# v from scaled raw x, the inverse rms behind its products, the shift's share behind attention, and h made later

## The chip, the cores and the metric

The kernel runs on one core of a Trainium2 chip. A core has TensorE (PE in the profile, its weight loads PEld), VectorE (DVE), ScalarE (ACT), GpSimd (POOL) and SyncE (SP, which issues most DMAs); each runs its own instructions in order, and semaphores tie them together. The metric is the time of one execution on the device in microseconds, the median of several.

## The reference

One layer of an encoder over 512 positions of width 1024 (DEPTH and BATCH are 1). What bears on the change is the head of it and one branch:

```python
mod = silu(c) @ w_c + b_c                      # 3 x 1024
shift, scl, gate = split(mod, 3)
h = rms_norm(x, g_pre) * (1.0 + scl) + shift   # 512 x 1024
proj = h @ w_in                                # 512 x 8192
xa, za, q, k, v, zb, ga, gb = split(proj)      # 1024 columns each
y_b = neighbourhood_attention(q, k, v, rpb) * silu(zb)
```

rms_norm multiplies each row of x by one number, the inverse of its root mean square. The other branch (a convolution, two recurrences over the positions), the two sigmoid gates, the three output products w_pa, w_pb, w_o and a last rms_norm follow. All is float32; the kernel makes a float32 product from three products of numbers split in a high and a low part (high x high, high x low, low x high), each rounded to the form that TensorE takes at full speed.

## The kernel before

`Plan` holds a list of operations, each with its engine, an estimated cost, the tiles it reads and writes and a rank. `Plan.run` emits them engine by engine: the lowest rank among those that can begin about now by its estimates. What it emits is the order of each engine's instructions; on the chip they run in that order and wait for their data. `HEAD` (line 44) gives ranks by name to the operations of the beginning. Tiles come from fixed sets of slots (36 of 128x512, 32 of 128x1024, eight PSUM banks).

The beginning, in the order of the data:

- `par_sb` (line 405) holds c and the small parameters; its DMA is issued by ScalarE. Line 409 to 417 make silu(c) in it and transpose it; line 437 writes silu(c), broadcast to 128 rows, into two PSUM banks `cbs` by 16 products; `silr` is its copy in SBUF (line 380, a helper for all copies and casts).
- `xT` (line 470) is x turned, features on partitions, four tiles of two feature slices each, loaded in two halves of 256 positions. Squares (line 483), their sums over slices (486, 490), the sums over partitions by products with ones (496) and `rstd_ops` (464 to 462) give the inverse rms of each position; line 513 broadcasts it to all partitions (`rb`, `rbs`).
- `modulate(k)` loads for each of eight feature slices k two tiles of w_c (`wc`) and reduces them against silu(c): scale `scs[k]`, with g_pre in it, and shift `shs[k]`. Slice 0 has forms of its own (551, 555), slice 1 reads PSUM in halves (566), the others read `silr` (571).
- `make_h(k)`: ht = xT x scale x inverse rms (584, 595), hh = ht + shift rounded (587, 598), hl the rest of it (589, 600).
- `split_v(k)`: `wv`, the rows of w_in that make v, as `vh` and `vl` (380, 620, 383).
- `vmm`: v in eight units, two halves of 512 columns times four blocks of 128 positions (`VU`), each in a PSUM bank `vps`; 8 units x 8 slices x 3 products = 192 products (line 386, a helper for all such products), slice by slice. `fill` (504) puts short products in TensorE's way before them, so that it isn't idle.
- `vout` (676, 677, 680): v is split in high and low and written to DRAM (`vscr`), from where attention loads it in another order (`load_v`).

Then `proj` makes one tile of 128 columns x 512 positions of any of the other projections: a load of 0.5 MB (`wraw`), a cast (`whi`, line 380), a subtraction (`wlo`, 383) and 24 products with hh and hl. For the first head pairs the order is q, k and the gate z; each further one follows in the same way. `bias` (738) makes the bias tables on POOL. `scores` and `attend` run for two head pairs at a time between the products of later projections. At its end `attend` writes the inverse sums of the softmax to DRAM and reads them back broadcast (905, 908, `rcx`), multiplies them into the gate sz (909), multiplies that by the attention output yt (911), and splits the result in `ybh` and `ybl` for the products with w_pb, which come after all attention. `gate_of` and `main` tie loads to the progress of TensorE.

## Time and profile before

| what | us |
|---|---|
| three timed runs | 558.68, 558.93, 559.44 |
| median | 558.93 |
| span of the profiled execution, from its first to its last instruction | 556.93 |
| TensorE busy in the span | 548.6 |
| VectorE, ScalarE, POOL busy | 388.4, 320.1, 102.1 |
| moved by DMA | 82.54 MB |

The profiled execution has no time of its own beside its span; the difference to the timed runs, about 2 us, is what lies before the first and behind the last instruction. A row of the timeline gives the start in us from the span's beginning, the duration in us (of several like instructions together, "x16"), the engine, the line, the operation, what it writes <- what it reads, the shapes, and in brackets the idle time ahead of it and who ended it. A row by groups gives the count, the total in us, the mean in ns and the idle time. SPq and ACTq are the instructions with which SP and ScalarE issue DMAs.

### The profile page before, as it was taken

The numbers are of one execution on the slowest core, as the hardware profiler recorded it, in microseconds if no ns is written. First come the engines' busy times: TensorE is split into PE (matmuls) and PEld (weight loads), VectorE is DVE, ScalarE is ACT, GpSimd is POOL, SyncE is SP. The second block draws the span as 40 slices with busy tenths as digits, with TensorE's granted clock in tenths as the row PEclk, the third lists the DMA queues.
The fourth block names the chain that finished last, engine by engine and source line by source line (L and its number), as shares of the span: only waits on it lengthen the run. The fifth ranks groups of instructions, "written<-read, shape, count | busy, mean of one in ns | idle before, by whom it ended". The sixth has DMA issues, their size and how long they took to land.

```text
span 556.9 us, 7643 instructions
## 1 busy us (share of the span) xinstructions
PE 548.6 (99%) x2769; PEld 458.8 (82%) x2769; DVE 388.4 (70%) x707; ACT 320.1 (57%) x557; POOL 102.1 (18%) x98
## 2 busy tenths in 40 slices
...
GB/s 294 408 408 124 299 302 198 155 191 54 148 202 67 123 200 114 4 95 190 78 123 159 31 122 167 41 114 62 89 100 376 130 76 75 152 301 1 0 38 115
DMA packets 30825, 82.54 MB, mean 148 GB/s; under 512 B 4548, under 2 KB 5700, under 8 KB 30788
## 3 DMA queue, kind: packets, MB, share of 16 engines
...
q14 instruction: 15, 0.12, 0.1%
HBM read 75.60 MB, written 6.44 MB: 147 GB/s over the span
## 4 chain that ended last, share of the span: by engine, by line
PE 99%; DVE 0%; POOL 0%; issue 0%; ACT 0%; POOLq 0%
PE acc L386 79%; PE hx L386 8%; PE pv L386 3%; PE pt L848 2%; PE sp L386 2%; PE gt L386 2%; PE hx L504 1%; PE hx L437 1%; PE hd L551 0%; PE hd L496 0%; PE hd L513 0%; DVE yo L1215 0%; DVE yo L1183 0%; DVE xr L1187 0%; ACT sd L1205 0%
## 5 line engine op out<-in xcount | busy, mean ns | idle before, releaser
L386 PE MATMUL acc<-hhl,whi 128*128 128x512 f32 x784 | 243.1, 391 | 0.0
L386 PEld LDWEIGHTS acc<-hhl,whi 128*128 128x128 f32 x784 | 145.7, 188 | 29.2
L386 PE MATMUL acc<-hhl,wlo 128*128 128x512 f32 x392 | 152.9, 390 | 0.0
L386 PEld LDWEIGHTS acc<-hhl,wlo 128*128 128x128 f32 x392 | 73.6, 188 | 15.5
L380 ACT CAST whi<-wraw 128x1024 fp32r<-128x1024 f32 x72 | 74.4, 1045 | 1.8 <-DMA wraw<-in_w_in_dram 0.9
L1194 POOL TENSOR_TENSOR yo<-yo,gfin 128x512 f32<-128x512 f32 x6 | 8.1, 1350 | 337.8 <-ACT xr L1191 337.7
L383 POOL TENSOR_TENSOR wlo<-wraw,whi 128x1024 fp32r<-128x1024 f32 x23 | 56.0, 2438 | 64.0 <-ACT whi L380 32.1
L383 DVE TENSOR_TENSOR wlo<-wraw,whi 128x1024 fp32r<-128x1024 f32 x49 | 59.2, 1220 | 2.3 <-ACT whi L380 2.1
L386 PE MATMUL acc<-woh,mhl 128*128 128x512 f32 (+1 forms) x144 | 40.4, 366 | 0.0
L386 PE MATMUL acc<-ybhl,whi 128*128 128x512 f32 x128 | 39.4, 390 | 0.0
L386 PE MATMUL acc<-yahl,whi 128*128 128x512 f32 x128 | 39.4, 390 | 0.0
L738 POOL TENSOR_TENSOR nb<-msk,braw 128x192 f32<-128x192 f32 (+1 forms) x48 | 30.7, 670 | 27.8 <-DMA braw<-in_rpb_dram 26.7
L837 ACT ACTIVATE p<-p,mn 128x192 f32<-128x192 f32 (+1 forms) x64 | 30.4, 478 | 6.7 <-DVE mn L830 6.6
L1079 DVE SCALAR_TENSOR_TENSOR gm<-gm,acc 128x512 f32<-128x512 f32 x16 | 11.0, 688 | 33.0 <-PE acc L386 33.0
L386 PE MATMUL hx<-vh,hhl 128*128 128x512 f32 x112 | 33.5, 389 | 0.0
L830 DVE CUSTOM_DVE_ANT_0 p<-sp,nb 128x192 f32<-128x192 f32 (+1 forms) x64 | 31.4, 602 | 0.6 <-PE sp L386 0.2
L386 PEld LDWEIGHTS acc<-woh,mhl 128*128 128x128 f32 x144 | 26.1, 189 | 4.4
L985 DVE SCALAR_TENSOR_TENSOR xc<-acc,prm,xc 128x511 f32<-128x511 f32 (+1 forms) x24 | 18.0, 750 | 14.9 <-ACT xc L978 14.3
L386 PEld LDWEIGHTS acc<-ybhl,whi 128*128 128x128 f32 x128 | 24.0, 188 | 5.0
L386 PEld LDWEIGHTS acc<-yahl,whi 128*128 128x128 f32 x128 | 24.0, 188 | 5.0
L386 PE MATMUL acc<-wol,mhl 128*128 128x512 f32 (+1 forms) x72 | 26.4, 366 | 0.0
L386 PE MATMUL acc<-yahl,wlo 128*128 128x512 f32 x64 | 24.9, 390 | 0.0
...
## 6 DMA issues: line engine op xcount, KB each, us to landing
wraw<-in_w_in_dram SPq DMA_DIRECT2D x56, 512.0 KB, 5.0
wc<-in_w_m_dram SPq DMA_DIRECT2D x22, 512.0 KB, 10.1
...
vscr<-va SPq DMA_DIRECT2D x8, 512.0 KB, 4.3
wraw<-in_w_pb_dram SPq DMA_DIRECT2D x8, 512.0 KB, 3.5
wraw<-in_w_pa_dram SPq DMA_DIRECT2D x8, 512.0 KB
wo<-in_w_o_dram SPq DMA_DIRECT2D x8, 512.0 KB, 5.2
wv<-in_w_v_dram SPq DMA_DIRECT2D x7, 512.0 KB
```

The lines of the kernel that those rows point to most:

```text
L380: return lambda e: nc.scalar.copy(o(), i()) if e == "ACT" else nc.vector.tensor_copy(o(), i())
L383: return lambda e: ENGINE[e].tensor_tensor(o(), a(), b().bitcast(F32), op=ALU.subtract)
L386: nc.tensor.matmul(o, a, b, start=first, stop=last)
L437: nc.tensor.matmul(cb.ap[:, k * P:(k + 1) * P], ident.ap[:, 4 * n + k:4 * n + k + 1].to_broadcast([P, P]), par_sb.ap, start=True, stop=True)
L504: op("PE", 0.3, lambda e: nc.tensor.matmul(wb.ap[:, :P], onesc.ap, onesc.ap, start=True, stop=True), 5000 + j, r=[onesc], hold=[wb], until ...
L738: nc.gpsimd.tensor_tensor(o, mv, view, op=ALU.subtract)
L830: nc.vector.tensor_tensor_reduce(out=o, in0=v(spv(h, e)[:, :nk]), in1=v(nb[:, h, :nk]), scale=1.0, scalar=3e38, op0=ALU.add, op1=ALU.min, ...
L837: nc.scalar.activation(pv2(i), pv2(i), AF.Exp, bias=mn.ap[:, c:c + 1], scale=-1.0, accum_out=sm.ap[:, 4 * h + b:4 * h + b + 1])
L848: nc.tensor.transpose(ptp.ap[:, j * P:(j + 1) * P], pt_.ap[:, j * P:(j + 1) * P], ident.ap)
L985: nc.vector.scalar_tensor_tensor(a, b, wcol, a, op0=ALU.mult, op1=ALU.add)
L1079: op("DVE", dve(512), lambda e: nc.vector.scalar_tensor_tensor(t.ap, t.ap, 1.0, o.ap, op0=ALU.add, op1=ALU.mult), n - 1.9, r=[o], rw=[t], ...
L1194: op(("DVE", "POOL"), (dve(w), pool_(w)), lambda e: ENGINE[e].tensor_tensor(y(), y(), gfin[n].ap[:, gs], op=ALU.mult), rank + 0.1, r=[gfin ...
```

## The change

v is no longer made from h. With r the inverse rms of a position, scale' = g_pre x (1 + scl) and s the shift, h = r x (x scale') + s, so v = r x (x scale') @ w_v + s @ w_v. The first part needs no r until after its products; the second is one number per column of v and, since the weights of the softmax sum to one, the same number per column of the attention output.

- `split_x(k)`: hx = xT x scale' rounded, lx the rest; the products of v take these. `modulate` is split in scale (m = 1) for all slices, then shift (m = 0); both are one reduction 1024 wide that reads silu(c) from two PSUM banks side by side (`pair`). The special forms of slices 0 and 1 go.
- The squares are now taken of x itself, positions on partitions: four tiles `xn` of 0.5 MB are loaded for it, ScalarE squares and sums each; root, reciprocal and one Newton step give r in `rxc`, one column per block of 128 positions. It is turned, written to DRAM and read back broadcast as `rbs` by two DMAs that ScalarE issues. The products of line 496, 513 and 551 go.
- `make_h` comes behind all that: POOL multiplies xT by `rbs` (ht), ScalarE applies scale and shift (hs) and rounds (hh), VectorE subtracts (hl).
- `split_v`: 512-wide casts; the subtractions of the second half (k > 0) go to POOL.
- Six of the eight units of v run slice by slice; the last two run all eight slices after them.
- `vout`: r is multiplied in while v is split, on ScalarE by its scale operand, on VectorE in two passes 256 wide.
- The shift's share: shift is turned, written to DRAM and read back broadcast (`shr`); for each head pair a turned tile `wvt` of w_v (0.5 MB, a new input) is loaded and reduced against it (`v_bias`). In `attend` szr and yb become ytr = yt x rcx and yb = (ytr + share) x sz.
- x_t is stored so that each load of `xT` is one of 0.5 MB. `HEAD` is new; `AFTER` is empty; `Plan` counts DMA at slightly other rates.

```diff
+    "mod11": -17.3886, "lx1": -17.2743, "vh31": -17.0702, "wv0": -16.5875, "wc01": -16.1285, "x0": -16.0517,
+    "hx0": -15.3174, "wv1": -15.269, "vl21": -15.2314, "rn": -15.1384, "lx2": -15.1381, "lx6": -15.0948,
+    "sq0": -15.0022, "vl30": -14.9726, "mod21": -14.9726, "rv": -14.958, "vh20": -14.9549, "vh01": -14.8259,
+    "rd": -14.8255, "hx1": -14.8111, "vl00": -14.7926, "rxs": -14.7914, "hx2": -14.7913, "sq2": -14.7906,
+    "vh10": -14.7903, "sq1": -14.7846, "vh11": -14.7845, "vl01": -14.7726, "wc11": -14.1485, "wv2": -14.1485,
+    "xn0": -14.1484, "hx7": -13.8386, "vl20": -13.755, "xn1": -13.425, "wc21": -13.4246, "x1": -11.5502,
+    "wv3": -10.6407, "wc31": -10.6405, "wv4": -10.6403, "x2": -10.6403, "wc41": -10.0318, "wc51": -9.4608,
+    "mod51": -9.2919, "xn3": -9.2864, "vl41": -8.7911, "vl60": -8.7248, "mod01": -8.5793, "rr": -8.5792,
+    "mod41": -8.579, "mod71": -8.5634, "vl31": -8.5632, "wlo11": -8.4861, "lx4": -8.3642, "mod61": -8.3639,
+    "lx0": -8.3637, "vl61": -8.3098, "wlo10": -8.3032, "lx3": -8.1603, "hx4": -8.1298, "mod31": -8.1233,
+    "vh70": -7.9037, "wv5": -7.7231, "hx6": -7.7091, "vl10": -7.6401, "silr1": -7.4727, "vh71": -7.4726,
+    "xn2": -7.4663, "wc61": -7.4659, "vh21": -7.3661, "whi11": -7.366, "wv6": -7.347, "hx5": -7.1954, "x3": -7.1314,
+    "vh60": -7.1263, "hx3": -7.1056, "vh50": -7.0646, "vh61": -7.0642, "silr0": -6.7343, "sq3": -6.7223,
+    "voh": -6.5563, "rxl": -6.4074, "vh41": -6.4073, "vh00": -6.4, "vh30": -6.0598, "vh40": -5.3971,
+    "wc71": -4.8311, "w10": -4.7451, "wv7": -4.6289, "wc10": -4.6288, "wc60": -4.6039, "vh51": -4.1781,
+    "wc00": -3.7535, "w9": -3.6762, "wc30": -3.6235, "wc20": -3.548, "w11": -3.1239, "wc70": -3.1235,
+    "wc50": -2.8074, "wc40": -2.807, "vl71": -2.4421, "vl11": -2.1401, "ht0": -2.1401, "ht3": -2.0073,
...
+    pair = ps.tile([P, 1024], F32, name="pair")
+
     def B(cls):
-        return pl.tile(cls, lambda i: ps.tile([P, 512], F32, tag=f"b{i}", name=nm(cls)))
+        return pl.tile(cls, lambda i: pair[:, 512 * i - 1024:512 * i - 512] if i in (2, 3) else ps.tile([P, 512], F32, tag=f"b{i}", name=nm(cls)))
...
-    xTp = {(j, i): xT[j].part(i * 512, i * 512 + 512) for i in range(2) for j in range(4)}
-    for i in range(2):
-        for j in range(4):
-            load(xTp[j, i], whole(xTp[j, i]), x_t[i, j], -19.9 + 0.4 * i + 0.1 * j, 262144, name=f"x{i}{j}")
+    for j in range(4):
+        load(xT[j], whole(xT[j]), x_t[j], -19.9 + 0.1 * j, 524288, spare=2, name=f"x{j}")
+
+    ssx, rxc, rxt = const("ssx", [P, NT]), const("rxc", [P, 32]), T("rxt")
+    op("POOL", 0.1, lambda e: nc.gpsimd.memset(rxc.ap, 1.0), 0, w=[rxc])
+    for t in range(NT):
+        xn = W("xn")
+        load(xn, whole(xn), x[t * P:(t + 1) * P, :], 0, 524288, spare=2, name=f"xn{t}")
+        op("ACT", act(1024, 0, True), lambda e, xn=xn, t=t: nc.scalar.activation(xn.ap, xn.ap, AF.Square, accum_out=ssx.ap[:, t:t + 1]), 0,
+           rw=[xn], w=[ssx], name=f"sq{t}")
+    rv, rsd, rrc, rq = (C(f"{g}2", NT, 1) for g in ("v", "sd", "r", "q"))
+
+    def newton(e):
+        nc.vector.tensor_tensor(rq.ap, rrc.ap, rrc.ap, op=ALU.mult)
+        nc.vector.tensor_tensor(rq.ap, rq.ap, rv.ap, op=ALU.mult)
+        nc.vector.scalar_tensor_tensor(rxc.ap[:, :NT], rq.ap, -3.0, rrc.ap, op0=ALU.add, op1=ALU.mult)
+        nc.vector.transpose(rxt.ap[:, :32], rxc.ap)
+
+    op("ACT", 0.29, lambda e: nc.scalar.activation(rsd.ap, ssx.ap, AF.Sqrt, bias=epsc.ap), 0, r=[ssx, epsc], w=[rsd], name="rd")
+    op("DVE", 0.17, lambda e: nc.vector.tensor_scalar(rv.ap, ssx.ap, D * EPS, None, op0=ALU.add), 0, r=[ssx], w=[rv], name="rv")
+    op("DVE", 0.17, lambda e: nc.vector.reciprocal(rrc.ap, rsd.ap), 0, r=[rsd], w=[rrc], name="rr")
+    op("DVE", 0.8, newton, 0, r=[rrc, rv], rw=[rxc], w=[rq, rxt], lock=True, name="rn")
+
+    def turned(scr):
+
+        return bass.AP(scr.tensor, scr.offset, [[32, 4], [P, 32], [1, 32]])
+
+    xscr = pl.fixed(dp.tile([32, P], F32, name="xscr"))
+    op("ACT", 0.5, lambda e: nc.scalar.dma_start(turned(xscr.ap), rxt.ap[:, :32]), 0, r=[rxt], w=[xscr], late=3.0, name="rxs")
+    rbs = T("rbs")
+    op("ACT", 0.5, lambda e: nc.scalar.dma_start(rbs.ap, bass.AP(xscr.ap.tensor, xscr.ap.offset, [[0, P], [1, 512]])), 0, r=[xscr], w=[rbs],
+       late=4.0, name="rxl")
...
+    hx, lx, hh, hl = {}, {}, {}, {}
+    vh, vl = {}, {}
+    shc, sht = const("shc", [P, 32]), T("sht")
+
+    def sil():
+        assert [cb.slot for cb in cbs] == [2, 3]
+        return pair
+
+    zero = op("POOL", 0.1, lambda e: nc.gpsimd.memset(shc.ap, 0.0), -18.5, w=[shc])
+
+    def modulate(k, m):
+
+        t, r = W("wc"), C("sc", 1, 10) if m else shc.part(k, k + 1)
+        (scs if m else shs)[k] = r
+        b = mods.ap[:, 8 + k:9 + k] if m else pc(16 + k, 17 + k)
+        g = mods.ap[:, k:k + 1] if m else 0.5
+        load(t, whole(t), w_m[3 * k + m], k - 5, 524288, spare=2, name=f"wc{k}{m}")
+        op("DVE", dve(1024) + 0.08, lambda e: nc.vector.tensor_tensor_reduce(
+            out=t.ap, in0=t.ap, in1=sil(), scale=g, scalar=b, op0=ALU.mult, op1=ALU.add, accum_out=r.ap),
+           k - 1.5, r=cbs + [mods, prm], rw=[t], w=[r], after=[zero], name=f"mod{k}{m}")
+
+    def split_x(k):
+
+        hx[k], lx[k] = two("xhl")
+        xk = lambda: xT[k // 2].ap[:, k % 2 * 512:k % 2 * 512 + 512]
+        op("ACT", act(512, 1), lambda e: nc.scalar.activation(hx[k].ap, xk(), AF.Copy, scale=scs[k].ap), k - 1.19,
+           r=[xT[k // 2], scs[k]], w=[hx[k]], name=f"hx{k}")
+        op("DVE", dve(512), lambda e: nc.vector.scalar_tensor_tensor(
+            lx[k].ap, xk(), scs[k].ap, hx[k].ap.bitcast(F32), op0=ALU.mult, op1=ALU.subtract), k - 1.18,
+           r=[xT[k // 2], hx[k], scs[k]], w=[lx[k]], lock=True, name=f"lx{k}")
...
+        xk = lambda: xT[k // 2].ap[:, k % 2 * 512:k % 2 * 512 + 512]
+        op("POOL", pool_(512), lambda e: nc.gpsimd.tensor_tensor(t.ap, xk(), rbs.ap, op=ALU.mult), k - 1.2, r=[xT[k // 2], rbs], w=[t], name=f"ht{k}")
+        op("ACT", act(512, 2), lambda e: nc.scalar.activation(t.ap, t.ap, AF.Identity, scale=scs[k].ap, bias=shs[k].ap), k - 1.195,
+           r=[scs[k], shs[k]], rw=[t], name=f"hs{k}")
+        op("ACT", act(512), cast(whole(hh[k]), whole(t)), k - 1.19, r=[t], w=[hh[k]], name=f"hh{k}")
+        op("DVE", dve(512), sub(whole(hl[k]), whole(t), whole(hh[k])), k - 1.18, r=[t, hh[k]], w=[hl[k]], lock=True, name=f"hl{k}")
...
+        t, z = W("wv"), (slice(0, S), slice(S, D))
+        load(t, whole(t), w_v[k], k - 4.5, 524288, spare=2, name=f"wv{k}")
+        (h0, l0), h1, l1 = two("vhl"), T("vh", F32R), T("vl", F32R)
+        for n, hi, lo in ((0, h0, l0), (1, h1, l1)):
+            vh[k, n], vl[k, n] = (hi, whole(hi)), (lo, whole(lo))
+            op("ACT", act(512), lambda e, hi=hi, n=n: nc.scalar.copy(hi.ap, t.ap[:, z[n]]), k - 1.1, r=[t], w=[hi], name=f"vh{k}{n}")
+            op(*(("POOL", pool_(512)) if k and n else (("DVE", "POOL"), (dve(512), pool_(512)))), sub(whole(lo), lambda n=n: t.ap[:, z[n]], whole(hi)), k - 1.09, r=[t, hi],
+               w=[lo], lock=True, name=f"vl{k}{n}")
 
     for k in range(KD):
-        modulate(k)
-        wv_load(k)
+        modulate(k, 1)
+        split_x(k)
+        split_v(k)
+    for k in range(KD):
+        modulate(k, 0)
         make_h(k)
...
-                mm(vps[u].ap, (hl if p == 2 else hh)[k].ap[:, ts], (vl if p == 1 else vh)[k, n][1](),
+                mm(vps[u].ap, (lx if p == 2 else hx)[k].ap[:, ts], (vl if p == 1 else vh)[k, n][1](),
                    k == 0 and p == 0, k == KD - 1 and p == 2)
-        th, tl = (hhp[t // 2], hlp[t // 2]) if k == 0 else (hh[k], hl[k])
+        th, tl = hx[k], lx[k]
...
+        for j, parts in enumerate(([0], [1], [2]) if k < 2 else ([0, 1], [2]) if k < KD - 1 else ([0, 1, 2],)):
+            for m, u in enumerate(VU[:6]):
+                ops.append(vmm(u, k, parts, k + 0.1 * j + 0.01 * m))
         main.append(ops[0])
         if k == 0:
-            fill(ops[12], vps[VU[2]])
+            fill(ops[5], vps[VU[5]])
+    for m, u in enumerate(VU[6:]):
+        ops = [vmm(u, k, [0, 1, 2], 8 + 0.2 * m + 0.01 * k) for k in range(KD)]
...
-        op("ACT", act(512), lambda e: nc.scalar.copy(view(0, 192), src()), rank, r=[vps[u]], w=[a], name="voh")
-        op("DVE", dve(512), lambda e: nc.vector.tensor_tensor(view(64, 64), src(), view(0, 192).bitcast(F32), op=ALU.subtract),
-           rank, r=[vps[u]], rw=[a], name="vol")
+        rs = rxc.ap[:, t:t + 1]
+        op("ACT", act(512, 1), lambda e: nc.scalar.activation(view(0, 192), src(), AF.Copy, scale=rs), rank, r=[vps[u], rxc], w=[a], name="voh")
+        def low(e):
+            for b in range(2):
+                o, i1 = (a.ap.rearrange("p (g c) -> p g c", g=4)[:, :, c:c + 64] for c in (64 + 64 * b, 192 * b))
+                nc.vector.scalar_tensor_tensor(o, src()[:, :, b, :], rs, i1.bitcast(F32), op0=ALU.mult, op1=ALU.subtract)
+        op("DVE", 2 * dve(256), low, rank, r=[vps[u], rxc], rw=[a], name="vol")
...
+    sscr = pl.fixed(dp.tile([32, P], F32, name="sscr"))
+    op("DVE", 0.2, lambda e: nc.vector.transpose(sht.ap[:, :32], shc.ap), 7, r=[shc], w=[sht], name="sht")
+    op("SP", 0.5, lambda e: nc.sync.dma_start(turned(sscr.ap), sht.ap[:, :32]), 8, r=[sht], w=[sscr], size=16384, late=SLACK, name="shs")
+    shr = W("shr")
+    load(shr, whole(shr), bass.AP(sscr.ap.tensor, sscr.ap.offset, [[0, P], [1, D]]), 8, 524288, r=[sscr], spare=3, name="shr")
+    cv = const("cv", [P, KD])
+    cvs = [cv.part(i, i + 1) for i in range(KD)]
+
+    def v_bias(pr, rank, after):
+
+        t = W("wvt")
+        load(t, whole(t), w_vt[pr], rank - 2, 524288, after=after, spare=5, name="wvt")
+        op("DVE", dve(1024) + 0.08, lambda e: nc.vector.tensor_tensor_reduce(
+            out=t.ap, in0=t.ap, in1=shr.ap, scale=0.5, scalar=0.0, op0=ALU.mult, op1=ALU.add, accum_out=cvs[pr].ap), rank,
+           r=[shr], rw=[t], w=[cvs[pr]], lock=True, name="cv")
...
-        op("DVE", dve(512), lambda e: nc.vector.tensor_tensor(rbc(sz.ap), rbc(sz.ap), nat(rcx.ap), op=ALU.mult),
-           pos - 0.3, r=[rcx], rw=[sz], lock=True, name="szr")
-        op("DVE", dve(512), lambda e: nc.vector.tensor_tensor(rbc(sz.ap), nat(yt.ap), rbc(sz.ap), op=ALU.mult), pos + 0.5, r=[yt],
-           rw=[sz], lock=True, name="yb")
+        v_bias(pr, pos + 0.2, gate_of(len(main), 2))
+        op("DVE", dve(512), lambda e: nc.vector.tensor_tensor(rbc(rct.ap), nat(yt.ap), nat(rcx.ap), op=ALU.mult),
+           pos + 0.4, r=[yt, rcx], rw=[rct], lock=True, name="ytr")
+        op("DVE", dve(512), lambda e: nc.vector.scalar_tensor_tensor(sz.ap, rct.ap, cvs[pr].ap, sz.ap, op0=ALU.add, op1=ALU.mult),
+           pos + 0.5, r=[rct, cvs[pr]], rw=[sz], lock=True, name="yb")
```

More of the change, by code (lines that the diff above doesn't have):

```diff
@@ L44 @@
 HEAD = {
[22 rows of a table removed]
-AFTER = [('wc71', 'wc41')]
[25 rows of a table added]
+}
+AFTER = []
 class Tile_:
@@ L334, in layer @@
 @with_exitstack
-def layer(ctx, tc, x, x_t, par, w_m, w_v, w_in, w_blk, rpb, amask, w_pa, w_pb, w_o, g_final, out):
+def layer(ctx, tc, x, x_t, par, w_m, w_v, w_vt, w_in, w_blk, rpb, amask, w_pa, w_pb, w_o, g_final, out):
     nc = tc.nc
```

156 lines of the change are left out of this document (4 added, 152 removed), and 30 rows, old and new, of the table HEAD.

## The prediction, made before the changed kernel was run

> **What bounds the kernel now.** First the page: its share of busy time and the chain that ended last.
>
> ```profile
> span 556.9 us, 7643 instructions
> PE 548.6 (99%) x2769; PEld 458.8 (82%) x2769; DVE 388.4 (70%) x707; ACT 320.1 (57%) x557; POOL 102.1 (18%) x98
> PE 99%; DVE 0%; POOL 0%; issue 0%; ACT 0%; POOLq 0%
> ```
>
> TensorE carries 99% of the chain, so the same chain in order of time is read next (start, us, what), to see which of its pieces are work and which only fill time.
>
> ```profile
> 5.09 2.99 PE hx L437 x16
> 8.08 2.46 PE hx L504 x22
> ...
> 16.34 44.23 PE hx L386 x192
> 60.57 19.49 PE acc L386 x86
> ...
> 397.22 152.89 PE acc L386 x696
> 550.11 0.02 issue
> ```
>
> Three stretches. Up to 16 us TensorE is busy, but with warm-up products (L504) and small products that prepare the inputs. Then come the 192 products of v until 60.57 us, then everything else until 550.1 us, back to back. One product of the projections costs 19.49/86 = 0.2266 us; 192 at that rate are 43.5 us. So the v stage, which takes 44.47 us from its first product at 16.10 (below) to 60.57, loses only 1.0 us. The kernel gains by starting v sooner and loses by any hole after it; faster helpers alone give nothing.
>
> The timeline shows what the first product of v waits for.
>
> ```profile
> 3.94 0.31 ACT L409 ACTIVATE tan<-par_sb 8x128 f32<-8x128 f32 x1 [1.26 <-DMA par_sb<-in_par_dram]
> 12.33 1.06 PE L496 MATMUL hd<-onesc,sq 128*128 128x64 f32 x8
> 13.37 0.16 DVE L462 SCALAR_TENSOR_TENSOR rx<-q,r 128x2 f32<-128x2 f32 x1
> 15.51 0.51 ACT L587 ACTIVATE hh<-ht,sh 128x256 fp32r<-128x256 f32 x1 [0.21 <-DVE ht L584]
> 16.10 0.71 PE L386 MATMUL hx<-vh,hh 128*128 128x512 f32 x2
> ```
>
> The broadcast silu(c) is ready when L437 ends, 5.09 + 2.99 = 8.08. From there to 16.10 pass squares of x, their sums (L496), the inverse rms (L462 and steps like it) and its broadcast, scale, shift, and hh (L587): h must be whole before v begins.
>
> **The change part by part.**
>
> *Start of v.* Its left operand becomes x times (1+scale), so squares, rms, broadcast and shift leave the path. What stays: L437 ends at 8.08, one reduction against silu(c) makes scale, one ScalarE pass makes hx, the product starts.
>
> ```profile
> 12.12 0.74 DVE L555 CUSTOM_DVE_ANT_0 wc<-wc,hx,prm 128x512 f32<-128x512 f32 x1
> 50.03 1.28 DVE L571 CUSTOM_DVE_ANT_0 wc<-wc,silr,prm 128x1024 f32<-128x1024 f32 x1
> 51.23 0.08 DVE L571 DVE_READ_ACCUMULATOR2_ANT sh<- 128x1 f32 x1
> L598 ACT ACTIVATE hhl<-ht,sh 128x512 fp32r<-128x512 f32 x7 | 5.1, 725 | 12.1 <-DVE ht L595 8.6 <-DVE sh L571 3.5
> L620 ACT CAST vh<-wv 128x512 fp32r<-128x512 f32 x2 | 1.1, 620 | 1.3 <-DMA wv<-in_w_v_dram 1.3
> ```
>
> The new reduction is 1024 wide with one input in two PSUM banks, which the trace lacks. Between L571 (1.28, both in SBUF) and two L555 (1.48) I take 1.33. Then 8.08 + 0.12 hand-over + 1.33 + 0.08 + 0.05 + 0.73 + 0.05 = 10.4 us. A cast of wv (0.62, L620) or a copy of silu(c) of the same width already running on ScalarE can stand before hx: 10.4 to 11.05, I take 10.7. **16.10 - 10.7 = 5.4 us sooner.**
>
> *Do its inputs arrive?* By the order of the new HEAD the loads of half a megabyte run wv0, wc01, x0, wv1, wc11, wv2, xn0, xn1, wc21, x1, ..., with wc31 12th, x2 14th, wv5 18th, xn2 19th, x3 22nd, wc71 23rd, wv7 25th, and the last shift slice, wc40, 35th. What SP moves, by stretch (the columns are busy times of the five engines, the clock, DMA share, GB/s):
>
> ```profile
> 4.00:6.00 2.00, 2.00 (x12) 1.96 (x11) 1.05 (x5) 1.97 (x4) 0.00 (x0) 1.00 1.05 323
> 6.00:8.00 2.00, 2.00 (x13) 2.00 (x13) 0.74 (x3) 1.96 (x5) 0.00 (x0) 1.00 0.98 363
> 8.00:10.00 2.00, 2.00 (x20) 2.00 (x19) 1.86 (x4) 2.00 (x5) 0.00 (x0) 1.00 0.86 229
> 20.00:22.00 2.00, 2.00 (x10) 1.68 (x10) 1.22 (x2) 1.08 (x2) 0.00 (x0) 1.00 1.01 404
> 30.00:35.00 5.00, 5.00 (x23) 4.14 (x22) 5.00 (x8) 1.44 (x2) 0.00 (x0) 1.00 1.03 408
> ```
>
> Some 2 MB are in by 8 us; at 406 GB/s 0.524 MB take 1.29 us, so load n lands near 8.3 + 1.29(n-4): wc01 and x0 before 8, x1 at 16.0, wv7 at 35.4, wc40 at 48.3. (The dip to 229 I do not carry over: loads twice as large keep SP ahead.) Six units make 18 products, 4.08 us, per slice k, so slice 2 is due at 10.7 + 8.2 = 18.9 (x1 plus 0.73 for hx: 16.8) and slice 7 at 39.3 (wv7 plus two casts and a 512-wide subtraction, 0.75 as L600 below: 37.4). Slack 2 us everywhere; the two units left over then run 48 products without new input. I put 0.5 us of holes (0 to 1, as before): v ends at 10.7 + 43.5 + 0.5 = 54.7, **5.87 us ahead of 60.57**.
>
> *h is made later.* Now the first projection, due at 54.7, waits for h. Its chain: row squares, inverse rms, two small DMAs on ScalarE's queue (write, then broadcast read), POOL's product ht, two ScalarE passes (hs, hh), VectorE's hl. The last xn slice lands at 27.7; a square twice as wide as L620 (1.24), a root and five small VectorE steps like L462 (0.16 each, with their hand-overs 1.5) take it to 30.5, with ScalarE occupied to about 31. The like round trip before, scratch write to the issue of its read, then the landing:
>
> ```profile
> 104.54 0.59 SPq L905 DMA_DIRECT2D rscr<-rct  x1
> 107.56 1.12 SPq L375 DMA_DIRECT2D rcx<-rscr  x2
> rcx<-rscr SPq DMA_DIRECT2D x16, 128.0 KB, 5.7
> ```
>
> Hence rbs at 31 + 3.0 + up to 5.7: 37 to 40, I take 39. From there VectorE and POOL must share:
>
> ```profile
> 53.70 1.21 DVE L383 TENSOR_TENSOR wlo<-wraw,whi 128x1024 fp32r<-128x1024 f32 x1
> 53.81 3.35 POOL L383 TENSOR_TENSOR wlo<-wraw,whi 128x1024 fp32r<-128x1024 f32 x1 [7.32 <-DVE hhl L600]
> 17.35 1.30 POOL L383 TENSOR_TENSOR vl<-wv,vh 128x512 fp32r<-128x512 f32 x1 [0.68 <-ACT vh L380]
> 17.92 0.81 DVE L566 CUSTOM_DVE_ANT_0 wc<-wc,hx,mods 128x512 f32<-128x512 f32 x1 [0.31 <-DMA wc<-in_w_m_dram]
> L383 POOL TENSOR_TENSOR wlo<-wraw,whi 128x1024 fp32r<-128x1024 f32 x23 | 56.0, 2438 | 64.0 <-ACT whi L380 32.1
> L600 DVE SCALAR_TENSOR_TENSOR hhl<-ht,sh,hhl 128x512 fp32r<-128x512 f32 x7 | 5.2, 745 | 0.0
> ```
>
> A POOL subtraction that usually takes 2.44 took 3.35 because VectorE's, with both inputs in SBUF, had begun 0.11 us earlier: 0.91 lost, the two ran one after the other. L566, one input in PSUM, ran beside POOL (0.81 and 1.30): the shift reductions, whose second input is PSUM now, I cost at no time of POOL. After 39 us the exclusive work is: POOL 8 ht at 1.29, one vl 1.29, one wlo 2.44 = 14.05; VectorE 8 hl at 0.70 (0.745 less the overlap of neighbours) and a wlo 1.21 = 6.8. **39 + 20.85 = 59.9.** The last h pair is due at 54.7 + 7 x 0.68 + 0.23 = 59.7. So it just fits; if that wlo waits, it ends at 57.4. I take a hole of 0.7 us (0 to 3). ScalarE's share (8 x (0.73 + 0.62), six voh at 0.73 (L598) and a cast twice as wide as L620 = 16.4 us) fits the same 20 us. VectorE's own account there: 6.8, eight shift reductions 10.6, the first three vol 2.9 (below), 20.3 of 20.7 us: as full as POOL's, a second reason for a hole between 0 and 3.
>
> The Trainium skill bears on this ("SBUF — State Buffer", section "Who interferes with whom"): a VectorE instruction with two SBUF inputs and a GpSimd one that reads SBUF exclude each other for a whole instruction, one with at most one SBUF input does not. The trace agrees (0.91 us lost; L566 beside POOL). By it the shift reductions stay out of the exclusive work and the sum is the one above; did the rule not hold for them, the time would be rival E's.
>
> *Two units of v later, two banks for silu(c).* Same products, other order: nothing on TensorE. The seventh unit needs a bank; the first unit ends near 40, its evacuation takes 0.73 + 0.96 (next part), so it is free at 42, before the six units end at 43.5.
>
> *Evacuation of v.* voh with a scale is 0.73 at most (L598) instead of 0.62; vol becomes two 256-wide passes (0.48 each by L584, next fence) instead of one 512-wide (0.75, L600): 8 x 0.21 = 1.7 us more on VectorE, half of it after 55 us.
>
> *Shift's share behind attention.* One turn and scratch round trip, one broadcast load, then for each of eight head pairs a load of 0.5 MB and a reduction of 1.28 (L571): 10.2 us of VectorE. szr becomes ytr, one for one, but now behind yt: 0.69 later, needed only by the w_pb products many units on. Where attention runs, DMA moves a quarter of what it can (104 GB/s below against 408 above), so these 4.7 MB hide. Where VectorE is fullest:
>
> ```profile
> 16.06 0.48 DVE L584 SCALAR_TENSOR_TENSOR ht<-xT,sc,hd 128x256 f32<-128x256 f32 x1
> 76.00:92.00 16.00, 16.00 (x72) 13.25 (x72) 2.07 (x3) 5.88 (x7) 13.31 (x14) 1.00 0.83 271
> 239.00:256.00 17.00, 17.00 (x91) 14.60 (x90) 16.05 (x31) 11.09 (x24) 0.00 (x0) 1.00 0.35 104
> 256.00:272.00 16.00, 16.00 (x86) 12.87 (x85) 7.64 (x13) 12.37 (x20) 0.00 (x0) 1.00 0.40 138
> ```
>
> VectorE is busy 16.05 of 17 there and 7.64 of 16 right after: one reduction more would push work back by 0.3 us at once and 1.3 at worst. On TensorE between 0 and 1.3; I take 0.15. POOL has its heaviest stretch (13.31 of 16) where VectorE does almost nothing, so what is pushed there has room.
>
> **Sum:** -5.87 + 0.7 + 0.15 = -5.0. The profiled span is 556.93, 2.0 below the median of 558.93 of the timed runs, whose own spread is 0.76; I take the 2.0 as unchanged. **558.93 - 5.0 = 553.9 us.**
>
> **The rivals.**
>
> *A: h takes over as the bound.* rbs at 42 instead of 39 (the read lands 5.7 after its issue, as rcx's, and the squares queue on ScalarE), with wlo ahead: 42 + 20.85 = 62.9, 3.2 us after the due time. 558.93 - 5.87 + 3.2 + 0.15 = 556.4. For it: the chain POOL, ScalarE, ScalarE, VectorE is full for 20 us. Against it: a free order can put the wlo last, worth 2.4.
>
> *B: v starves.* If loads run at 363 GB/s, as between 6 and 8 us, not 406, one takes 1.44: wv7 lands at 38.5, its halves are ready at 40.5, 1.2 us after 39.3. With 0.6 for casts that stand in the way: 558.93 - 5.0 + 1.8 = 555.7. Against it: from 20 us on every stretch before shows 404 or more.
>
> *C, slower: the round trip of rbs falls behind SP's backlog.* A load of the stage lands 10 us after its issue:
>
> ```profile
> wc<-in_w_m_dram SPq DMA_DIRECT2D x14, 512.0 KB, 10.1
> ```
>
> If the write and the broadcast read of rbs on ScalarE's queue each wait that long, rbs is there at 31 + 20.2 + 1 = 52, h at 73, 13.3 us late: 558.93 - 5.87 + 13.3 + 0.15 = 566.5. It decides from rbs at 45: there the hole eats the 5.9 us. For it: the same engines carry both. Against it: par_sb, issued on ScalarE's queue beside SP's loads, was there by 3.94 us. The Trainium skill ("DMA: Bandwidth & Descriptors", section "Queues, rings and completion order") has each DMA engine take packets from its queues in turn, which also speaks against C; with so early a load no run here shows it under a full backlog.
>
> *D: v doesn't start sooner.* If ScalarE spends its time on the squares of xn and the casts of wv first, or x0 lands late, the first product stays near 15 or 16 and the kernel ends where it was, 558.7. Against it: of ScalarE's passes only two copies and four casts can be ready by 8.3 us, 3.7 us of work, most of it done before scale is; they put hx to about 11 us at worst.
>
> *E, slower too: reductions from two PSUM banks hold the port.* Then the eight shift reductions (8 x 1.33 = 10.6) join the exclusive work: h at 70.5, 10.8 us late, 564.0. L566 (0.81 beside POOL, 0.74 alone) speaks against it.
>
> **How the numbers follow.** Forecast 0.62 (own range 552.0 to 555.9); A 0.15; B 0.08; D 0.07; C 0.05; E 0.03. The earliest end is v at 10.4, no holes: 53.9, 6.6 ahead, 552.3, less 0.3 of scatter: 552.0. Upwards the range takes in B and A with 0.8 for their sizes: 557.2. Left out: C, D, E and tails, under 0.2. A change under 0.2% (1.1 us) can't be told from none. Faster: forecast, A, B = 0.85. Same: D = 0.07. Slower: C, E = 0.08.
>
> **What would show it.** The first v product near 10.7, 192 products over some 44 us, projections from 54.7. Right on the start but wrong on h: gaps before L386 acc<-hhl late in the first projection, released by VectorE's hl. B: gaps in hx products released by vh, vl or hx, ScalarE waiting on DMA. C: ht waiting on rbs after 45. D: the first hx product after 14. E: POOL's ht longer than 2 us beside the reductions. Wrong altogether if the 397 to 550 us stretch changes in length.

## The result, and the profile after

| | before | after |
|---|---|---|
| median of the timed runs, us | 559.18 (558.68 to 560.26) | 587.71 (587.01 to 588.61) |
| ratio after / before | | 1.0509, 95% interval 1.049 to 1.0528 |
| span of the profiled execution | 556.9 | 585.2 |
| first product of v starts | 16.10 | 11.53 |
| first product of the projections starts (v is done) | 60.57 | 57.33 |
| first product of the attention scores starts | 93.1 | 102.5 |
| from there to the end of the span | 463.8 | 482.7 |

The change is slower by 28.5 us; 553.9 was forecast, range 552.0 to 557.2. Of the medians further down, that of `both` is over four runs, of which one took 1414 us; its other three took 565.4 to 566.9. First the page of after: span, busy times, granted clock of TensorE in 40 slices of the span (9 is 0.9 or more of full speed), shares of the chain. The same rows of before, but for the clock, stand at the head of the prediction; before's clock is 9 in all slices but the last, an 8.

```profile
span 585.2 us, 7603 instructions
PE 555.0 (95%) x2717; PEld 453.9 (78%) x2717; DVE 402.6 (69%) x714; ACT 328.3 (56%) x575; POOL 126.4 (22%) x115
PEclk9999979999999999999999999999999999999999
PE 80%; DMA 7%; DVE 6%; ACT 3%; issue 2%; POOL 1%; SPq 0%; DVEq 0%; ACTq 0%
```

TensorE carried 99% of the chain before and carries 80% now: it waits for DMA, VectorE and ScalarE. It issues fewer products and is yet busy longer (555.0 us; two_banks below, with the same 2717 products, is busy for 542.9); one slice of the clock is below full. The loss has two places, which the first score product divides (tile sp; name, count, duration in ns least/median/most, first and last start). Before:

```profile
L386 PE MATMUL sp<-kh,qh x64: 245/278/357, 93.1 to 224.4; 64*128 64x192 f32 x32, 64*128 64x256 f32 x32
```

After:

```profile
L393 PE MATMUL sp<-kh,qh x48: 246/278/357, 102.5 to 241.2; 64*128 64x256 f32 x26, 64*128 64x192 f32 x22
```

9.4 us are lost ahead of it and 18.9 behind it, in the stretch where the prediction had put 0.15. (The tile's name covers 48 of the 64 products in after: the other 16 write the tile `pair`, none of them before 102.5.) What TensorE waits for there (the view of waits: engine, tile, line <- engine waited for; us in all, times, longest). Before it has one row, 1.5 us for POOL ahead of the warm-up products. After:

```profile
PE acc L393 <- DVE hhl L390: 3.9, 2, 2.9
PE pair L393 <- DVE mn L773: 2.8, 4, 0.7
PE pair L393 <- ACT ri L959: 2.3, 3, 0.8
PE pair L393 <- DVE yt L827: 1.7, 3, 0.7
PE pair L393 <- DVE pp L801: 1.7, 2, 1.0
PE pair L393 <- ACT pp L799: 1.2, 2, 0.6
```

The row to stumble over is `pair`. It is the tile of two PSUM banks that the change made so that one reduction can read silu(c) in both. But `B` also hands its halves out, as banks 2 and 3, to everything that comes later: projections, scores, attention. The rows say that a product into `pair` waits for mn, ri, yt or pp, steps of attention and of the recurrences which don't feed it. They are readers of the other half. The timeline shows one such step and the product in the middle of a projection that waits for it, VectorE first:

```profile
198.84 0.63 DVE L773 CUSTOM_DVE_ANT_0 p<-pair,nb 128x256 f32<-128x256 f32 x1 [0.58 <-PE pair L393]
199.53 0.73 PE L393 MATMUL pair<-hhl,whi 128*128 128x512 f32 x2 [0.73 <-DVE mn L773]
```

(It reads `hhl`, a slice k > 0 of h, so it is not the first of its projection; mn is written by the second part of the step that reads `pair`.) Before has no such wait. With the rows not shown here, the products and transposes into `pair` have 21 waits of 14.4 us in all, two of them, of 1.5 us, ahead of the scores. The rest of the 18.9 us is not split up further.

The head has its own story. Start and end of v, and the last low parts of h:

```profile
9.37 1.34 DVE L522 CUSTOM_DVE_ANT_0 wc<-wc,pair,mods 128x1024 f32<-128x1024 f32 x1 [1.00 <-ACT silr L387]
11.53 1.20 PE L393 MATMUL hx<-vhl,xhl 128*128 128x512 f32 x4 [0.84 <-ACT xhl L530]
57.33 0.39 PE L393 MATMUL acc<-hh,whi 128*128 128x512 f32 x1
70.35 0.50 PE L393 MATMUL acc<-hhl,whi 128*128 128x512 f32 x1 [2.89 <-DVE hhl L390]
```

(The third row is the first product of the projections.) And why h is late, from the chain in order of time (start, us):

```profile
32.76 6.46 DMA xscr<-rxt
39.24 5.61 DMA rbs<-xscr
```

and from the timeline of ScalarE and POOL:

```profile
39.72 0.72 ACT L530 ACTIVATE xhl<-xT,sc 128x512 fp32r<-128x512 f32 x1 [4.04 <-DMA xscr<-rxt]
44.92 7.58 POOL L541 TENSOR_TENSOR ht<-xT,rbs 128x512 f32<-128x512 f32 x6 [1.94 <-DMA rbs<-xscr]
66.27 6.81 DVE L390 TENSOR_TENSOR hhl<-ht,hhl 128x512 fp32r<-128x512 f32 x4
67.36 5.17 POOL L390 TENSOR_TENSOR wlo<-wraw,whi 128x1024 fp32r<-128x1024 f32 x2
```

The inverse rms is there at 44.9, not 39; ScalarE stands 4 us ahead of the last slice's hx and casts, because the instruction that issues the read of `rbs` waits for the write; and four low parts of h take 6.81 us beside two low weight parts on POOL. From the first ht (44.92) to the end of the last low part (73.08) pass 28.2 us, for which the prediction had 20.85.

### The profile page after: what moved, and what is told of

The parts are those of the page before. It is cut to its first block, busy times and chain, and to the rows that moved or that the text cites. A ratio compares the mean times of both kernels' runs of the same rounds, so it can differ in the third digit from the quotient of the medians.

```text
span 585.2 us, 7603 instructions
## 1 busy us (share of the span) xinstructions
PE 555.0 (95%) x2717; PEld 453.9 (78%) x2717; DVE 402.6 (69%) x714; ACT 328.3 (56%) x575; POOL 126.4 (22%) x115
## 4 chain that ended last, share of the span: by engine, by line
PE 80%; DMA 7%; DVE 6%; ACT 3%; issue 2%; POOL 1%; SPq 0%; DVEq 0%; ACTq 0%
PE acc L393 51%; PE pair L393 23%; DMA xn<-in_x_dram 2%; PE pv L393 2%; DMA wv<-in_w_v_dram 2%; DVE hhl L390 2%; PE pt L791 2%; PE sp L393 1%; POOL ht L541 1%; DMA xscr<-rxt 1%; DMA rbs<-xscr 1%; DMA xT<-in_x_t_dram 1%; ACT ri L959 1%; ACT ri L956 1%; DVE va L609 0%
## 5 line engine op out<-in xcount | busy, mean ns | idle before, releaser
L393 PE MATMUL acc<-hhl,whi 128*128 128x512 f32 x518 | 162.9, 395 | 3.9 <-DVE hhl L390 3.9
L393 PEld LDWEIGHTS acc<-hhl,whi 128*128 128x128 f32 x518 | 97.8, 190 | 25.0 <-DVE hhl L390 4.9
L393 PE MATMUL acc<-hhl,wlo 128*128 128x512 f32 x259 | 101.9, 393 | 0.0
L393 PE MATMUL pair<-hhl,whi 128*128 128x512 f32 x266 | 85.4, 403 | 10.9 <-ACT ri L959 2.3
L393 PEld LDWEIGHTS pair<-hhl,whi 128*128 128x128 f32 x266 | 49.0, 191 | 27.1 <-ACT ri L959 3.6
L393 PEld LDWEIGHTS acc<-hhl,wlo 128*128 128x128 f32 x259 | 49.3, 190 | 10.5
L393 PE MATMUL pair<-hhl,wlo 128*128 128x512 f32 x133 | 52.6, 396 | 0.0
L393 PEld LDWEIGHTS pair<-hhl,wlo 128*128 128x128 f32 x133 | 25.3, 190 | 5.6
L393 PE MATMUL hx<-vhl,xhl 128*128 128x512 f32 x96 | 25.0, 393 | 1.8 <-ACT xhl L530 0.8
L393 PE MATMUL acc<-ybhl,wlo 128*128 128x512 f32 x64 | 24.9, 389 | 0.0
```

The lines of the kernel that those rows point to most:

```text
L393: nc.tensor.matmul(o, a, b, start=first, stop=last)
```

## The experiments

All runs with medians in us, ratio to before with its interval, and from the profile the start of the first score product, the span, and the difference of the two:

| kernel | median | ratio | score | span | behind |
|---|---|---|---|---|---|
| two_banks | 564.5 | 1.0096 (1.0069 to 1.0123) | 97.0 | 560.1 | 463.1 |
| before_pair | 568.0 | 1.016 (1.0145 to 1.0176) | 94.9 | 566.5 | 471.6 |
| rbs_free | 559.7 | 1.001 (0.9994 to 1.0025) | 95.7 | 558.7 | 463.0 |
| wlo_memset | 558.7 | 1.0 (0.999 to 1.0009) | 93.8 | 556.9 | 463.1 |
| wlo_dve | 559.7 | 1.0013 (1.0003 to 1.0022) | 95.4 | 558.5 | 463.1 |
| rxl_pool | 565.8 | 1.0122 (1.0106 to 1.0138) | 100.6 | 563.7 | 463.1 |
| both | 566.1 | 1.0129 (1.0106 to 1.0151) | 100.4 | 563.6 | 463.2 |
| late_issue | 562.2 | 1.0061 (1.0047 to 1.0075) | 97.5 | 560.6 | 463.1 |
| late_vol | 564.7 | 1.0102 (1.0087 to 1.0117) | 95.5 | 562.6 | 467.1 |
| rbs_fill | 558.3 | 1.0 (0.9991 to 1.0009) | 93.3 | 556.3 | 463.0 |

(In before_pair the first score product writes `pair`.) The last column is worth a look first: with the common tile gone it is 463.0 to 463.2 whatever the head does (before: 463.8), except in late_vol, which is explained there. So a change of the head shows in the total in full.

### The common tile

**two_banks**: after, with two banks of their own; each reduction in two halves, same order on every engine.

```diff
-    pair = ps.tile([P, 1024], F32, name="pair")
...
-        return pl.tile(cls, lambda i: pair[:, 512 * i - 1024:512 * i - 512] if i in (2, 3) else ps.tile([P, 512], F32, tag=f"b{i}", name=nm(cls)))
+        return pl.tile(cls, lambda i: ps.tile([P, 512], F32, tag=f"b{i}", name=nm(cls)))
...
+            for j, z in enumerate((slice(0, 512), slice(512, 1024))):
+                nc.vector.tensor_tensor_reduce(out=t.ap[:, z], in0=t.ap[:, z], in1=cbs[j].ap, scale=g, scalar=u if j else b,
+                                               op0=ALU.mult, op1=ALU.add, accum_out=r.ap if j else u)
```

> The changed kernel in the same order of instructions on every engine, but silu(c) in two separate bank tiles as before (no common tile 'pair'); each of the 16 reductions is two of 512. Theory A (what is written to one half of the common tile waits for whoever still reads the other half: 18.9 us of the 28.5 lie behind the first score product, 482.7 us from there to the end against 463.8 before): the stretch from the first score product to the end falls to 463 to 467, the waits of TensorE there vanish, and the whole takes 568 to 572 us. Rival B (VectorE's extra work in attention, the shift's share, or an order planned for other times): the stretch stays at 480 or more, the whole at 586 to 589.

**before_pair**: before, with the common tile and nothing else of the change (the two lines above, put into before).

> The kernel before, same order of instructions, with nothing changed but that banks 2 and 3 are the halves of one common tile. Theory A: TensorE gets waits in the middle of a projection that it has nowhere now; 5 to 20 us slower, 564 to 579. Rival B: the common tile costs nothing, 558.5 to 560.

Measured: 587.7 falls to 564.5 without the tile, and before rises from 558.9 to 568.0 with it. The waits of before_pair have the same form, in a kernel that has nothing else of the change:

```profile
PE pair L388 <- DVE mn L832: 1.9, 3, 0.7
PE pair L388 <- ACT pp L858: 0.7, 1, 0.7
```

So 23.2 of after's 28.5 us are the tile. Behind the first score product alone the two differ by 19.6 us (482.7 and 463.1), and with 463.1 two_banks is back at before's 463.8: nothing else of the change loses time there. The stretch is where theory A had it; the total is 3.5 us below its range, as the tile also cost 5.5 us ahead of the scores (102.5 and 97.0), which A had left out. That the tile costs 23.2 in one kernel and 9.2 in the other goes with the waits into `pair`: 21 of 14.4 us in after, 8 of 4.7 us in before_pair. Why after has more of them is not shown. The wait comes from the program, not from data: the two halves are two banks, and what reads one and writes the other shares no data. Order is kept by tiles, and `pair` is one tile.

### What holds up the head

two_banks still loses 5.6 us where 5.0 were to be won. Its timeline (an inner hole of v, its end, the last low parts of h, the hole behind them, the first scores):

```profile
41.78 0.50 PE L391 MATMUL hx<-vhl,xhl 128*128 128x512 f32 x1 [1.45 <-ACT vhl L555]
58.92 0.39 PE L391 MATMUL acc<-hh,whi 128*128 128x512 f32 x1
67.01 6.82 DVE L388 TENSOR_TENSOR hhl<-ht,hhl 128x512 fp32r<-128x512 f32 x4
71.09 0.50 PE L391 MATMUL acc<-hhl,whi 128*128 128x512 f32 x1 [2.89 <-DVE hhl L388]
97.02 0.36 PE L391 MATMUL sp<-kh,qh 64*128 64x192 f32 x2
```

**rbs_free**: two_banks, with the read of `rbs` fed from a row of x, so that nothing waits for the inverse rms. The kernel leaves the inverse rms out of h.

```diff
-    op("ACT", 0.5, lambda e: nc.scalar.dma_start(rbs.ap, bass.AP(xscr.ap.tensor, xscr.ap.offset, [[0, P], [1, 512]])), 0, r=[xscr], w=[rbs],
+    op("ACT", 0.5, lambda e: nc.scalar.dma_start(rbs.ap, bass.AP(x.tensor, x.offset, [[0, P], [1, 512]])), 0, r=[xscr], w=[rbs],
```

> As two_banks, but the broadcast read that fills rbs reads a row of x and so waits for nothing: the inverse rms is left out of h. rbs is there some 4 to 5 us sooner (near 40 instead of 44.9). Theory C (the late round trip bounds h): the first score product comes 3.5 to 5 us sooner than in two_banks, total 564 to 567. Rival D (the order on VectorE and the port shared with POOL bound h): less than 1.5 us sooner, 567 to 572.

**wlo_memset**: two_banks, with the low weight parts of the fourth and fifth projection written by a memset. The kernel leaves these low parts out.

```diff
-        op(engs, costs, sub(whole(low), whole(raw), whole(hi)), n - 2.1,
+        op(engs, costs, (lambda e: nc.gpsimd.memset(low.ap.bitcast(F32), 0.0)) if n in (12, 13) else sub(whole(low), whole(raw), whole(hi)), n - 2.1,
```

> As two_banks, but the two subtractions of 1024 on POOL that run while the last four hl are due (those of the fourth and fifth projection) are memsets, which read no SBUF: their low weight parts are left out. Rival D (hl waits for POOL at the shared port: 6.81 us for four hl instead of 2.8): the four take 3 us or less, the hole of 2.9 us goes, the first score product comes 2.5 to 5 us sooner than in two_banks. Theory C (only the late rbs counts): less than 1 us.

Without the wait for the inverse rms v ends 3.1 us sooner and POOL's ht starts at 40.67, yet the four low parts take as long as before:

```profile
55.79 0.39 PE L391 MATMUL acc<-hh,whi 128*128 128x512 f32 x1
40.67 7.57 POOL L542 TENSOR_TENSOR ht<-xT,rbs 128x512 f32<-128x512 f32 x6
63.25 6.82 DVE L388 TENSOR_TENSOR hhl<-ht,hhl 128x512 fp32r<-128x512 f32 x4
```

The first score product is only 1.3 us sooner than in two_banks (95.7 and 97.0), which looks like theory D. But the two profiled runs differ in TensorE's clock: its mean is 0.998 in that of two_banks and 0.992 in that of rbs_free, where the clock falls right behind the hole (the last group of experiments). Ahead of that fall, the product that waits for the first of the last low parts starts at 67.33, in two_banks at 71.09: 3.76 us sooner. Runs of like clock say the same: two_banks took 561.9 at 0.998 and a median of 564.6 in its three others, rbs_free a median of 558.4 in its five runs at 0.996 or more and 560.5 in its five others, 3.5 and 4.1 us less. So the late inverse rms costs about what theory C said. (Both totals expected were too high, as two_banks itself had been expected at 568 to 572.)

With POOL writing only, the four low parts take 2.49:

```profile
67.35 2.49 DVE L388 TENSOR_TENSOR hhl<-ht,hhl 128x512 fp32r<-128x512 f32 x4
68.42 1.84 POOL L634 MEMSET wlo<- 128x1024 f32 x2
93.81 0.36 PE L391 MATMUL sp<-kh,qh 64*128 64x192 f32 x2
```

4.33 us of VectorE's 6.82 were thus spent behind POOL: VectorE's subtraction of two tiles in SBUF and POOL's reads take turns. It is the rule that the prediction took from the Trainium skill ("SBUF — State Buffer", section "Who interferes with whom"), which states besides that POOL's writes alone don't count; the two rows agree, 6.82 beside two subtractions and 2.49 beside two memsets. The prediction counted one such subtraction on POOL until h is whole; four ran in after, two among the ht and two beside the last four low parts of h. The first score product comes 3.2 us sooner than in two_banks, and the total is 3.2 us below two_banks' run at full clock (558.7 and 561.9), as theory D had it. So the two causes weigh about the same; no run takes both away, so whether they add is not shown.

**wlo_dve**: two_banks, with the same two low weight parts on VectorE, behind the low parts of h.

```diff
-            q = proj(w_in[16 + pr], hhl, hll, LO_A if pr else "DVE")
-            k = proj(w_in[24 + pr], hhl, hll, LO_A)
+            q = proj(w_in[16 + pr], hhl, hll, LO_A if pr > 1 else "DVE")
+            k = proj(w_in[24 + pr], hhl, hll, "DVE" if pr == 1 else LO_A)
```

> As two_banks, but the low weight parts of the fourth and fifth projection are made by VectorE, behind the last hl, instead of by POOL: nothing is left out. Theory D (the shared port): the last four hl take 3 us or less instead of 6.8, the hole of 2.9 us before the product that needs them goes, total 558 to 561. Rival (VectorE is then too full): 562 or more.

```profile
68.45 3.44 DVE L388 TENSOR_TENSOR hhl<-ht,hhl 128x512 fp32r<-128x512 f32 x4
70.86 0.50 PE L391 MATMUL acc<-hhl,whi 128*128 128x512 f32 x1 [1.18 <-DVE hhl L388]
```

3.44 instead of 6.82, a hole of 1.18 instead of 2.89, 559.7 instead of 564.5. The total is as expected; the four low parts stay above the 3 us expected, the hole shrinks but doesn't go, and another of 1.87 us appears, where TensorE waits for a low weight part on VectorE. (Of the 4.8 us some 2.5 are TensorE's clock, which most runs of two_banks lost behind the hole: three of its four took 564.4 to 565.6 at a mean clock of 0.989 or 0.992, the profiled one 561.9 at 0.998.) With the whole computation in it this is the best form of the change found: 0.13% slower than before (0.03 to 0.22%), which is no gain.

**rxl_pool**: two_banks, with the read of `rbs` issued by POOL, so that ScalarE doesn't stand. **both**: the same with wlo_dve's edit.

```diff
-    op("ACT", 0.5, lambda e: nc.scalar.dma_start(rbs.ap, bass.AP(xscr.ap.tensor, xscr.ap.offset, [[0, P], [1, 512]])), 0, r=[xscr], w=[rbs],
+    op("ACT", 0.5, lambda e: nc.gpsimd.dma_start(rbs.ap, bass.AP(xscr.ap.tensor, xscr.ap.offset, [[0, P], [1, 512]])), 0, r=[xscr], w=[rbs],
```

> As two_banks, same order, but the broadcast read of rbs is issued by POOL, so that ScalarE no longer stands waiting for the scratch write with casts and hx behind it (4.0 us idle at 39.7). Theory C1 (this wait makes the holes in v: v takes from 10.86 to 58.92, 4.6 us over 43.5): v ends at 55.5 to 57, the total 561 to 563. Rival: the holes come from late loads; v ends at 58.5 or more, total as two_banks, 563 to 566.

> rxl_pool and wlo_dve together. If the two causes are independent: two_banks less both gains, 554.5 to 558; if ending v sooner only makes the wait for h longer: 557 to 561.

Both totals missed. In rxl_pool v ended early, as the theory said (first product behind it at 55.92), but POOL issued later and the data landed later still:

```profile
41.59 0.70 POOL L491 DMA_DIRECT2D rbs<-xscr  x1 [4.84 <-DMA xscr<-rxt]
48.34 7.55 POOL L542 TENSOR_TENSOR ht<-xT,rbs 128x512 f32<-128x512 f32 x6 [4.73 <-DMA rbs<-xscr]
60.00:65.00 5.00, 3.35 (x7) 1.99 (x7) 4.96 (x7) 2.32 (x5) 4.92 (x4) 0.50 0.60 241
```

ht starts 2.8 us later than in two_banks (45.53). The third row is a stretch of the span (busy times of PE, PEld, VectorE, ScalarE, POOL, then the granted clock, DMA share, GB/s): TensorE runs at half its clock here.

**late_issue**: wlo_dve, with the read issued on ScalarE behind the three operations that stood behind it. **late_vol**: late_issue, with the last eight low parts of v behind the last low parts of h; it holds them back in the way that is shown for the read.

```diff
+        if o.name == "rxl":
+            self.held = o
...
+        if o.name == "vh71":
+            self.held.fn("ACT")
```

> wlo_dve, with the read of rbs issued on ScalarE behind the three operations that stood behind it (the cast of x's eighth slice and the two casts of w_v's eighth pair) instead of ahead of them. Theory (ScalarE standing at the issue for the scratch write makes v's holes): the three are over before the write lands, so rbs still lands at 44.5 to 46, and the last product of v is at 55.6 to 56.5 instead of about 59, as where the wait is absent (rbs_free 55.79). The eight low parts of v ahead of the last low parts of h start up to 3 us sooner; the first score product moves from 95.38 to 92.5 to 95, the total from 559.7 to 556.8 to 559.3. Rival (the last low parts of h are bound by rbs and the rows of h, not by v's end): v ends at 56, the first score product stays at 95 to 95.6 and the total at 559 to 560.

> late_issue, with the eight low parts of v's last four units (3.18 us of VectorE in the after-like order) put behind the last low parts of h and the first of the two low weight parts, instead of ahead of them; nothing else of any engine's order changes. Theory (the end of the head is VectorE's chain up to the last low part of h): the last low parts of h start up to 3.2 us sooner than in late_issue, the hole ahead of their products (1.18 in wlo_dve) goes, the first score product is at 91 to 93.5 and the total at 554.5 to 558. Rival (the rows of h arrive late from POOL and ScalarE, so VectorE would have waited there anyway): less than 0.7 us sooner than late_issue at the first score product and in the total.

Both missed again. In late_issue v's holes go (the projections start at 55.78) and POOL's ht starts at 45.65, as expected, but VectorE falls behind POOL at two other places: two low parts of h take 4.55 us, and a small step of the recurrences' constants 3.42 beside POOL's bias table. VectorE:

```profile
56.05 4.55 DVE L393 TENSOR_TENSOR hhl<-ht,hhl 128x512 fp32r<-128x512 f32 x2
67.70 3.42 DVE L458 SCALAR_TENSOR_TENSOR lt<-prm 128x16 f32<-128x16 f32 x1
```

POOL:

```profile
57.39 2.66 POOL L393 TENSOR_TENSOR wlo<-wraw,whi 128x1024 fp32r<-128x1024 f32 x1
67.68 3.40 POOL L671 TENSOR_TENSOR nb<-msk,braw 128x256 f32<-128x256 f32 x6
```

The one small step stands through all six of POOL's operations; in wlo_dve, where it met the end of such a row of operations, the same step took 0.19.

In late_vol the scores start 2.0 us sooner than in late_issue, less than the theory had (91 to 93.5 was expected, 95.5 measured); the stretch behind them grows by 4.0. SP's queue waits (one row of its waits) for the low parts of v that it writes out. Further rows: a reduction of the shift's share, and a score product:

```profile
SPq L626 <- DVE va L623: 9.1, 4, 8.0
97.66 1.62 DVE L717 CUSTOM_DVE_ANT_0 wvt<-wvt,shr 128x1024 f32<-128x1024 f32 x1 [0.51 <-DMA wvt<-in_w_vt_dram]
99.94 0.39 PE L404 MATMUL sp<-kh,qh 64*128 64x256 f32 x1 [1.98 <-DVE sz L850]
```

For 8 us SP issues nothing, so the loads behind it come later. VectorE waits for one of them, the gate's step sz comes behind that reduction, and TensorE stands 1.98 us for sz in the scores; from 101.19 to 104.60 its clock is at 0.50. The head is thus tight on three sides (ScalarE's queue, the port that VectorE and POOL share, SP's queue): what each edit won at its own place was lost at the next.

### The clock

**rbs_fill**: rbs_free, with ten idle products in the places where TensorE stood. Like rbs_free, the kernel leaves the inverse rms out of h.

```diff
+                mm(o.ap, a, rh[k][1](), k == 0, False)
+                for _ in range({4: 8, 6: 2}.get(k, 0) if n == 9 else 0):
+                    nc.tensor.matmul(cbs[1].ap[:, :P], onesc.ap, onesc.ap, start=True, stop=True)
+                mm(o.ap, a, rl[k][1](), False, False)
```

> rbs_free (in which the inverse rms is left out of h) with ten idle products of 128x128 on TensorE, whose results nobody reads, put ahead of the two products that waited for a low part of h: eight ahead of the first (its hole was 2.88 us), two ahead of the second (0.85). One takes about 0.3 us by the rows at the start, so they fill 2.4 and 0.6 us of time that TensorE stood anyway. Theory (the granted clock of 0.73 in the stretch from 70 to 80 us comes from TensorE's hole, not from other engines): the clock is 1.00 there, products take 0.39 instead of 0.63 each, the first score product moves from 95.70 to 92.5 to 94.5, and the total from 559.7 to 556.5 to 558.7. Rival (the clock falls there for another reason, or VectorE's low parts set the pace anyway): the clock stays at 0.70 to 0.80 in that stretch, or it is 1.00 but new holes behind VectorE take the gain; the first score product is at 95 to 96.5 and the total at 559 to 561.

rbs_free (the product behind the hole, and the stretch behind it):

```profile
67.33 0.50 PE L391 MATMUL acc<-hhl,whi 128*128 128x512 f32 x1 [2.88 <-DVE hhl L388]
69.00:75.00 6.00, 5.15 (x13) 3.83 (x13) 5.59 (x14) 1.53 (x2) 5.06 (x8) 0.50 0.97 255
```

rbs_fill (the eight idle products ahead of the first, two records each; the same product, the stretch, the scores):

```profile
64.30 1.95 PE L641 MATMUL hx<-onesc 128*128 128x128 f32 x16
67.33 0.50 PE L391 MATMUL acc<-hhl,whi 128*128 128x512 f32 x1 [1.08 <-DVE hhl L388]
67.00:75.00 8.00, 6.97 (x31) 5.67 (x32) 7.76 (x10) 2.13 (x3) 8.00 (x8) 1.00 1.01 290
L391 PE MATMUL sp<-kh,qh x64: 246/277/356, 93.3 to 224.4; 64*128 64x192 f32 x32, 64*128 64x256 f32 x32
```

The awaited product starts at 67.33 in both, so the idle products moved no data any sooner. The clock behind it is 1.00 instead of 0.50, and the scores start at 93.3 instead of 95.7, as the theory expected (92.5 to 94.5). TensorE's own hole had lowered its clock, and that cost 2.4 us. By medians it is 1.4 (559.71 and 558.30), because the clock doesn't fall in each run of rbs_free: in five of its ten the mean clock was 0.996 or 0.998 and the time 557.9 to 559.3, in five 0.991 to 0.993 and 560.1 to 561.3. The median of the first five, 558.4, is that of rbs_fill: the idle products gain what the clock had cost, and no more.

## Why the prediction was wrong, step by step

*Start of v*: right. 11.53 against 10.7, in two_banks 10.86; the reduction from two banks took 1.34 (1.33 taken). In after it starts late, at 9.37, behind the copy of silu(c) by ScalarE, one more wait that goes with the common tile: in two_banks the first half of it starts at 8.29.

*Do its inputs arrive?* The loads did: no hole in v is released by a load. But v ended at 57.3 (58.9 in two_banks) instead of 54.7. The holes came from ScalarE, which stood 4.04 us (4.60 in two_banks) at the issue of `rbs` with casts of v queued behind. The prediction's 0.5 us of holes did not ask what is queued behind that issue. rbs_free and late_issue show it: without that stand v ends near 56.

*h is made later*: the order of events was rival C's, at half its delay: rbs came 5.9 us after the 39 taken, where C had 13. The write was issued at 32.8 (31 assumed), and the round trip took 6.46 and 5.61 us, against 3.0 and up to 5.7 assumed. The row of 3.0 came from a stretch where the DMA share was 0.37 (104 to 108 us in before); during the write it was 0.90. That the loads beside it slowed the write, as C says, fits but was not tested. With rbs at 44.9 it reached just the point (45) from which C was to decide. The step failed a second time in its account of the port, 28.2 us where 20.85 were taken: it counted one low weight part on POOL, but four ran until h was whole, the last two beside the last four low parts of h (6.82 instead of 2.49), and the low parts of v stood ahead of those.

*Two units of v later, two banks for silu(c)*: the step that decided. "Same products, other order: nothing on TensorE" priced the bank's turn-over in the head and not what a tile of two banks does to its users afterwards. It measured 23.2 us. The line that tells it, `pair[:, ...] if i in (2, 3)`, was in the diff; no rival was made of it. Nor would the prediction's last sign, the stretch from 397 us on, have told of it: from the last product into gt to the end of the span pass 160.1 us in before (from 396.8) and 161.0 in after (from 424.2), so the tile's loss lies almost all between the first score product and there.

*Evacuation of v*: eight passes took 3.18 us, 0.40 each where 0.48 was taken. That four units of it stand ahead of the last low parts of h was not seen; late_vol shows 2.0 us for it at the scores, given back behind SP's queue.

*Shift's share*: right. Behind the first score product two_banks takes 463.1 us and before 463.8, so it cost nothing there that shows; 0.15 was an upper bound.

Rivals B and D didn't occur, and E is refuted: the reduction took 1.34 with a source of two banks, and the six ht on POOL, with shift reductions beside them, 7.58 us, 1.26 each. A and C had the right place, the head's end behind h, and C the right sign.
